# Loading the first w_down block of the first down phase one pair sooner, into the free half of s3

## The chip, the cores and the metric

One core of one Trainium2 chip. The metric is device time in microseconds (us), as the median of several executions; lower is better. The profile's own span leaves out some 1.8 us of that time, so spans are compared with spans and times with times. Engines are called TensorE (PE in the profile, PEld for its weight loads), DVE, ScalarE (ACT), GpSimd (POOL) and SyncE (SP, or SPq for its DMA queue).

## The reference

A gated MLP on 8 x 1024 tokens, with a hidden size of 1024 and an intermediate size of 4096, all float32:

```python
gate = x @ w_gate
up = x @ w_up
gate = 0.5 * gate * (1 + np.tanh(np.sqrt(2 / np.pi) * (gate + 0.044715 * gate ** 3)))
h = gate * up
return (h @ w_down).astype(np.float32)
```

## The kernel before

The kernel works through 8 passes of 1024 tokens in float16, with fast (Strassen-like) matrix products. Pass 0 has 16 "pairs" of gate and up products (56 matmuls of 512 columns in each but the first, which is built differently), then a down phase of 14 "blocks" (32 matmuls of 512 columns each): 7 products, two blocks of w_down operands for each. In pass 0 the even blocks are loaded from a DRAM scratch `wdop`, and the odd blocks are held on chip. The loads use six slots of 4096 columns in `rg`, the ring:

```python
def d_place(p, k):
    if p == 0:
        return (4, 2, 3, 5, 4, 5, 4)[k // 2]     # blocks 0,2,4,6,8,10,12
    return order[0][k % 6]

def d_chunk(p, k):
    if p == 0 and k % 2:
        return half_block(k // 2)
    o = 4096 * d_place(p, k)
    return rg[:, o : o + 4096].rearrange("p (n h) -> p n h", n=8)
```

Slot 4 also holds weight sums of every even pair, so block 0 can be loaded into it only after pair 14. The load is put into the program in pair 15 (`at(k, f, ...)` calls f after the k-th product of the pair):

```python
if i == NP - 1:
    at(1, load_d, p, 2 if p else 0)
```

The tile `s3` (8192 columns) first stages w_down while `wdop` is made; the last stores from it are issued in pass 0 near 174 us. In the down phase it takes the difference a11 - a21, in four quarters r, which the fifth product (P7, from block 8 on) reads:

```python
def hsum(o, a, b, op, r):
    s = slice(4 * r, 4 * r + 4)
    nc.vector.tensor_tensor(hq[o][:, s, :], hq[a][:, s, :], hq[b][:, s, :], op)

for r in range(4):
    sums["P1", 0, r] = [("s3", "a11", "a21", SUB, r)]     # in block 0, after row group r
    sums["P1", 1, r] = [("a21", "a21", "a22", ADD, r)]    # in block 1
```

The same phase makes more operands on DVE: sums for the odd blocks (line 461, stored to `wd_ops` by SyncE) and, for later passes, "quad sums" of w_down (line 278, stored to `wd_quads` by SyncE). It also fetches the next pass's x with four DMA transposes:

```python
if nb == 0 and g == 0 and p + 1 < NPASS:
    ...
    if v == (3 - p if p < FAST - 1 else 0):    # pass 0: in block 6
        transpose_x(p + 1)
...
load_d(p, kc + 6 if p else {0: 8, 6: 10, 8: 12}.get(kc, 14))    # at the end of block kc
```

SyncE issues all of these from one queue, in program order.

## Time and profile before

| what | before |
|---|---|
| time, median of 3 runs | 2256.03 us (2255.78 to 2256.38) |
| span of the profiled run (a run of 2255.39 us) | 2253.6 us |
| TensorE busy | 2245.6 us |
| TensorE's waits in the whole span | 3.8 us |
| of these in the first down phase | 0.6 us, at block 10 |
| block 0's load | issued 197.20, landed 203.6, needed at 209.1 |

TensorE is busy for all but a few microseconds, so a change can save time only where TensorE waits. The lines that show this are in the prediction below.

### The profile page before, as it was taken

How to read it: one execution, taken by the hardware profiler on the slowest of the kernel's cores; microseconds unless marked ns; L12 is line 12 of the kernel's file. 1: busy time of each engine (PE TensorE's matmuls, PEld its weight loads, DVE VectorE, ACT ScalarE, POOL GpSimd, SP SyncE). 2: the span in 40 equal slices, each digit the busy share in tenths (PEclk: the TensorE clock that was granted, in tenths of full speed). 3: DMA queues.
4: the chain of work that ended last, by engine and by line, in shares of the span. 5: the costliest groups of instructions: out<-in, count | busy, mean ns of one | idle time of the engine just before them, and what ended most of it. 6: DMA issues, size and time to landing. Idle time of an engine off the chain costs nothing.

```text
span 2253.6 us, 42764 instructions
## 1 busy us (share of the span) xinstructions
PE 2245.6 (100%) x16616; PEld 1624.2 (72%) x16616; DVE 1565.1 (69%) x2187; ACT 955.4 (42%) x1863; POOL 674.6 (30%) x825
## 2 busy tenths in 40 slices
PE   9999999999999999999999999999999999999999
PEld 4444444444444445888888888888888888888888
DVE  6666458883588755877776677666786667866674
ACT  4443135651365622666125550356404653055520
POOL 1332013330133300555014540255403543044520
PEclk9999999999999999999999999999999999999999
DMA  9898969999999999999998999988998889998886
GB/s 243 164 210 215 289 180 243 258 270 291 243 229 249 281 304 352 332 343 366 302 337 276 320 309 310 324 267 328 314 322 314 283 310 317 322 309 276 285 292 225
DMA packets 309117, 642.46 MB, mean 285 GB/s; under 512 B 79088, under 2 KB 185328, under 8 KB 288368
## 3 DMA queue, kind: packets, MB, share of 16 engines
q1 hardware_dynamic: 254128, 566.57, 73.5%
q0 software_dynamic: 54784, 73.14, 19.5%
q8 instruction: 130, 2.13, 0.4%
q14 instruction: 75, 0.61, 0.1%
HBM read 574.36 MB, written 138.41 MB: 316 GB/s over the span
## 4 chain that ended last, share of the span: by engine, by line
PE 87%; DMA 2%; SPq 1%; DVE 0%; issue 0%; DVEq 0%
PE ps L857 40%; PE ps L1108 20%; PE ps L635 17%; PE ps L1000 10%; DMA wd_quads<-x_sums 1%; SPq L255 0%; DMA ring<-wd_ops 0%; DVE x_sums L278 0%; DVE h_a L932 0%; DVE tmp L1177 0%; SPq L496 0%; DVEq L278 0%; SPq L544 0%
## 5 line engine op out<-in xcount | busy, mean ns | idle before, releaser
L857 PEld LDWEIGHTS <-ring 128*128 128x128 f16 x8320 | 814.1, 98 | 94.4
L834 POOL TENSOR_TENSOR h_a<-tmp 128x256 f16<-128x256 f32 x640 | 468.0, 750 | 840.6 <-ACT tmp L822 833.5
L857 PE MATMUL ps<-x_sums,ring 128*128 128x256 f16 x5760 | 655.8, 273 | 0.0
L819 DVE TENSOR_TENSOR tmp<-tmp,ps 128x512 f32<-128x512 f32 x640 | 414.3, 683 | 147.1 <-PE ps L857 90.2
L635 PEld LDWEIGHTS <-ring 128*128 128x128 f16 x2632 | 257.4, 98 | 311.2 <-DVE ring L360 0.9
L804 ACT COPY tmp<-ps 128x512 f32<-128x512 f32 x520 | 304.2, 585 | 237.0 <-PE ps L857 163.3
L635 PE MATMUL ps<-x_sums,ring 128*128 128x512 f16 x1504 | 340.1, 379 | 0.2 <-DVE ring L360 0.2
L822 ACT ACTIVATE tmp<-tmp 128x256 f32<-128x256 f32 x640 | 263.7, 418 | 173.2 <-DVE tmp L817 79.5
L857 PE MATMUL ps<-x_b,ring 128*128 128x256 f16 x2560 | 305.6, 273 | 0.0
L817 DVE TENSOR_TENSOR tmp<-ps,tmp 128x512 f32<-128x512 f32 x240 | 165.4, 689 | 145.2 <-ACT tmp L804 99.8
L635 PE MATMUL ps<-x_b,ring 128*128 128x512 f16 x1128 | 259.1, 379 | 0.0
L661 POOL TENSOR_TENSOR h_a<-tmp 128x512 f16<-128x512 f32 x94 | 141.1, 1501 | 377.4 <-ACT tmp L659 265.3
L1108 PEld LDWEIGHTS <-h_a 128*128 128x128 f16 x2240 | 219.2, 98 | 25.3
L1000 PE MATMUL ps<-ring,h_a 128*128 128x512 f16 x1024 | 222.3, 379 | 0.6 <-DMA ring<-wd_ops 0.6
L1108 PE MATMUL ps<-ring,h_a 128*128 128x256 f16 x1920 | 216.1, 273 | 0.0
L1000 PEld LDWEIGHTS <-h_a 128*128 128x128 f16 x1152 | 112.6, 98 | 136.8 <-DMA ring<-wd_ops 1.1
L654 DVE TENSOR_TENSOR tmp<-ps,tmp 128x512 f32<-128x512 f32 x188 | 127.3, 685 | 108.0 <-ACT tmp L646 106.5
L1165 ACT ACTIVATE tmp<-ps 128x512 f32<-128x512 f32 x60 | 35.3, 597 | 362.6 <-PE ps L1108 274.6
L1177 DVE SCALAR_TENSOR_TENSOR tmp<-ps,tmp 128x512 f32<-128x512 f32 x120 | 81.1, 690 | 97.5 <-PE ps L1108 66.7
L360 DVE TENSOR_TENSOR ring<-ring 128x1024 f16<-128x1024 f16 x188 | 139.7, 757 | 11.7 <-DMA ring<-in_w_up_dram 7.5
L646 ACT COPY tmp<-ps 128x512 f32<-128x512 f32 x188 | 109.8, 586 | 77.8 <-PE ps L635 77.8
L1108 PE MATMUL ps<-ring,x_sums 128*128 128x256 f16 x1120 | 126.3, 273 | 0.0
(102 smaller groups left out, 1534.0 us busy)
## 6 DMA issues: line engine op xcount, KB each, us to landing
ring<-w_ops SPq DMA_DIRECT2D x480, 512.0 KB, 4.9
ring<-wd_quads SPq DMA_DIRECT2D x110, 1024.0 KB, 6.9
ring<-wd_ops SPq DMA_DIRECT2D x35, 1024.0 KB, 8.2
out_dram<-tmp SPq DMA_DIRECT2D x128, 256.0 KB, 6.6
w_ops<-h_s SPq DMA_DIRECT2D x128, 256.0 KB, 6.8
ring<-in_w_gate_dram POOLq DMA_DIRECT2D x23, 1024.0 KB, 10.6
ring<-in_w_up_dram POOLq DMA_DIRECT2D x23, 1024.0 KB, 17.9
wd_quads<-x_sums SPq DMA_DIRECT2D x131, 128.0 KB, 6.5
```

The source lines that it names most:

```text
L360: nc.vector.tensor_tensor(o, a, b, op)
L635: nc.tensor.matmul(ps(b, w), lhs[:, k], rhs[:, k, :], start=(first and k == 0), stop=(k == KH - 1), skip_group_check=True,)
L654: nc.vector.tensor_tensor(o, ps("b", w), o, ADD)
L661: nc.gpsimd.tensor_tensor(hq[TO[n]][:, i, :], tmp[:, t[n, 1]], tmp[:, t[n, 0]], MUL)
L804: nc.scalar.copy(tmp[:, t[o[1]]], ps_all[:, bank[o[2]]])
L817: nc.vector.tensor_tensor(d, b, a, SUB)
L819: nc.vector.tensor_tensor(d, a, b, ADD if o[4] == "add" else SUB)
L822: nc.scalar.activation(d, d, GELU, scale=GSC)
L834: nc.gpsimd.tensor_tensor(h, tmp[:, t[o[1]], MQ : 2 * MQ], g, MUL)
L857: nc.tensor.matmul(ps_all[:, bank[c], w * MQ : (w + 1) * MQ], lhs[:, w, k], rhs[:, k], start=(first and w == 0 and k == 0), stop=(k == KH ...
L1000: nc.tensor.matmul(ps_all[:, bank[b, g]], lhs[:, j, g * P : (g + 1) * P], dc[:, n, :], start=(first and j == 0), stop=(j == NP - 1), skip_ ...
L1108: nc.tensor.matmul(ps_all[:, bank[c], m * MQ : (m + 1) * MQ], lhs[:, j, m * P : (m + 1) * P], rhs[:, j, :], start=(first and j == 0 and m ...
```

## The change

The intent is to give the first load of the down phase more time. Block 0 no longer goes to ring slot 4 but to the upper half of s3, which staging has left, and its load is put into pair 14. Two of the four a11 - a21 sums write that half, so they move behind block 0. The diff, without the blank lines that it adds:

```diff
     def d_chunk(p, k):
         if p == 0 and k % 2:
             return half_block(k // 2)
+        if p == 0 and k == 0:
+            return hf["s3"][:, 4096:8192].rearrange("p (n h) -> p n h", n=8)
         o = 4096 * d_place(p, k)
...
             if i == NP - 2:
                 order[0] = [0, 1, 4, 2, 3, 5] if p % 2 == 0 else [2, 3, 4, 0, 1, 5]
+                at(2, load_d, p, 0)
                 if p:
-                    at(2, load_d, p, 0)
                     at(3, load_d, p, 1)
-            if i == NP - 1:
-                at(1, load_d, p, 2 if p else 0)
+            if i == NP - 1 and p:
+                at(1, load_d, p, 2)
...
         for r in range(4):
-            sums["P1", 0, r] = [("s3", "a11", "a21", SUB, r)]
-            sums["P1", 1, r] = [("a21", "a21", "a22", ADD, r)]
+            late = p == 0 and r > 1
+            sums.setdefault(("P1", int(late), r % 2 if late else r), []).append(
+                ("s3", "a11", "a21", SUB, r)
+            )
+        for r in range(4):
+            sums.setdefault(("P1", 1, r), []).append(("a21", "a21", "a22", ADD, r))
```

## The prediction

> **What bounds the kernel now.** I read the page's busy list first, then the list of what TensorE waited for, then TensorE's timeline across the first down phase, then the chain of waits there, and last the DVE and SyncE order in it. The busy list, and the whole of TensorE's waits in the kernel (columns: total us, times, longest us):
>
> ```profile
> PE 2245.6 (100%) x16616; PEld 1624.2 (72%) x16616; DVE 1565.1 (69%) x2187; ACT 955.4 (42%) x1863; POOL 674.6 (30%) x825
> ...
> PE ps L1227 <- DVE h_s L1230: 1.6, 1, 1.6
> PE ps L314 <- DVE h_a L304: 0.7, 1, 0.7
> PE ps L1206 <- ACT x_b L317: 0.7, 1, 0.7
> PE ps L1000 <- DMA ring<-wd_ops: 0.6, 1, 0.6
> PE ps L635 <- DVE ring L360: 0.2, 1, 0.2
> ```
>
> The reader is to see that TensorE waits 3.8 us in all (1.6 + 0.7 + 0.7 + 0.6 + 0.2) in a span of 2253.6 us. The change touches only the first down phase (line 1000, pass 0), so all that it can remove from TensorE's path is the one wait of 0.6 us. The question is then whether that wait is the one for the first block. TensorE's timeline says no (start, length, what, idle before):
>
> ```profile
> 206.51 2.75 PE L635 MATMUL ps<-x_b,ring 128*128 128x512 f16 x12
> 209.10 7.07 PE L1000 MATMUL ps<-ring,h_a 128*128 128x512 f16 x32
> 216.00 7.07 PE L1000 MATMUL ps<-x_sums,h_a 128*128 128x512 f16 x32
> ...
> 278.93 20.89 PE L1000 MATMUL ps<-ring,h_a 128*128 128x512 f16 x96 [0.60 <-DMA ring<-wd_ops]
> ```
>
> The first block's 32 matmuls follow the last pair of gate and up with no gap: 206.51 plus 12 matmuls at 0.216 us is 209.10. The idle of 0.60 us stands at 278.93. A block of 32 matmuls takes 216.00 - 209.10 = 6.90 us, and (278.33 - 209.10) / 6.92 = 10.0, so the block that is late is number 10 of 0 to 13, not number 0. Its chain, traced back:
>
> ```profile
> 258.34 0.44 DVE x_sums L278
> ...
> 270.25 0.05 issue
> 270.30 0.02 SPq L544
> 270.32 0.03 issue
> 270.35 8.53 DMA ring<-wd_ops
> 278.88 0.05 issue
> 278.93 27.80 PE ps L1000 x128
> ```
>
> Block 10's load issues at 270.35, behind four transposes (259.17 to 270.25) in SyncE's queue, which stand behind the stores of w_down's quad sums (wd_quads), whose sums DVE makes. That chain goes back, over three landings of wd_quads stores (8.76, 9.70 and 8.77 us), to DVE at 228.96, where DVE had been busy back to back since 209. So DVE's pace from 209 to 232 sets the only wait in this phase.
>
> The first block's own load, in the DMA view of the instant it was issued (197.20; size, us to landing):
>
> ```profile
> ring<-wd_ops SPq DMA_DIRECT2D x1, 1024.0 KB, 6.4
> ```
>
> It landed at 197.2 + 6.4 = 203.6, and was needed at 209.1: 5.5 us to spare.
>
> **What the Trainium skill says.** (1) "TensorE: Matmul & The Clock Gate", section "Step-by-step: what each phase is for", gives 216 ns between back-to-back 512-column matmuls; here 32 take 6.90 us, 215.6 ns each. It agrees, so these blocks run at full pace with nothing to win inside them. (2) "DMA: Bandwidth & Descriptors", section "Anatomy of one DMA", says that DMA engines do not wait on semaphores: the wait is made on the issuing sequencer before dispatch. So a load put earlier in program order can go no sooner than its own waits let SyncE past, and whatever follows in that queue waits with it. The trace agrees: block 10's load goes 0.1 us after the last transpose ahead of it. (3) "SBUF — State Buffer", section "SBUF: two separate sides", says that compute and DMA sides do not contend there. So it should not matter to TensorE whether the block lies in the ring or in s3; no run so far tests that.
>
> **The change part by part.**
> (a) The first load moves from pair 15 to pair 14, and from ring slot 4 to the upper half of s3. Before, it had to wait for pair 14 to end (issued 197.20). Now it waits for the last stores of w_down staging: those issued at 173.28 and 174.48 took 9.9 and 10.4 us, so the last lands at 174.48 + 10.4 = 184.9. The DMA engines are almost empty then (2% from 184.9 to 190.0), and 4.9 us is the fastest this 1 MB load took here, so it should land near 190. The slack grows from 5.5 to about 19 us. TensorE did not wait on it: worth **0 us**.
> (b) Ring slot 4 is free early, so block 8's load no longer waits for block 0 (issued 216.20 before); it goes right behind block 6's, near 209.6. Block 8 is needed at 209.1 + 8 x 6.91 = 264.4, and its load landed at 221.1 even before. Worth 0 us. It takes 1 MB out of 216 to 221 and puts it among three other loads, 205.8 to 218, the first of which is needed only at 222.9.
> (c) TensorE, ScalarE and GpSimd keep their instructions and their order. On DVE no instruction is added, but two of the four a11-a21 sums (128x2048, 1.21 us, spaced 1.14 us) move behind block 0, because they write the half of s3 that block 0 now lies in. DVE's order before:
>
> ```profile
> 213.25 1.21 DVE L461 TENSOR_TENSOR x_sums<-x_sums 128x2048 f16<-128x2048 f16 x1
> 214.38 2.35 DVE L932 TENSOR_TENSOR h_s<-h_a,h_a 128x2048 f16<-128x2048 f16 x2
> 216.65 1.21 DVE L461 TENSOR_TENSOR x_sums<-x_sums 128x2048 f16<-128x2048 f16 x1
> 217.79 1.21 DVE L932 TENSOR_TENSOR h_a<-h_a,h_a 128x2048 f16<-128x2048 f16 x1
> ```
>
> In the changed order the second L461 sum comes up to 214.38 and is done by 215.5. The next is an a11-a21 sum, which may start only when TensorE has finished block 0. When that is seen, the kernel before shows: block 8's load waited for the same event and issued at 216.20. So DVE stands idle 216.20 - 215.51 = **0.69 us**, then runs the same work in nearly the same order: the a21 sums, from 217.79, start at about 217.3 for the first and 0.7 us late from the second on. All that DVE made later, up to 232, is 0.7 us later.
> (d) The consumers on TensorE do not notice. P6 reads the a11 sums from block 4 (236.7), and they begin at 225.94 and end at 231.6, then 232.3; P7 reads s3 from block 8 (264.4), and its last sum ends at about 220.
> (e) The chain to block 10 does notice, since it starts in that DVE stretch. If the landings in it keep their length, block 10's load issues 0.7 us later (271.0), and TensorE's wait grows from 0.6 to 1.3 us.
> The sum: 0 (a) + 0 (b) + 0 (d) + 0.7 at most (e). The chain's links wait on busy DMA queues, and a store that issues 0.7 us later need not land that much later; I take **+0.5 us**, 2256.03 + 0.5 = 2256.5 us.
>
> **The rivals.**
> 1. The transfer was hidden anyway and nothing else moves: 2256.0. For it: no gap at 209.10. Against it: DVE has a new hole, in a stretch that heads the chain.
> 2. The emptier DMA queue helps: with 1 MB gone from 216 to 221, the wd_quads stores land sooner, and block 10 is in time. It can give back at most the 0.6 us: 2255.4. For it: landings of 8 to 10 us for 128 KB are queueing. Against it: the chain's slow stores start at 230, 9 us after that load had landed.
> 3. A new wait on the a21 or a11 sums or on s3 stops TensorE, or SyncE's queue jams on the early load: some us more. Against it: the margins in (d) are 4.4 us (block 4) and more, and nothing stands behind the early load in SyncE's queue until 205.84, 21 us after it can go.
> 4. The intent holds: a wait at the start of the phase goes, worth microseconds. Against it: there is none in the trace, and 45 us (2%) would be twelve times all of TensorE's waits.
>
> **Range and chances.** The runs before lie within 0.6 us (2255.78 to 2256.38). A chain of three queued landings can shift by a microsecond either way, but a gain is capped at 0.6 us while a loss is not. With half a microsecond more for another run of the chip, that gives 2254.8 to 2258.5. Over 2% either way needs a mechanism that no view shows: 0.005 each, and 0.99 for within 2%.
>
> **What would show it.** In the changed profile: block 0's load issued near 185 and landed near 190; no gap at the first line-1000 matmul, as before; block 8's load near 209.6; a DVE idle of about 0.7 us ended by TensorE just after 216; the wait for wd_ops at block 10 at 0.6 to 1.3 us, still TensorE's only wait in the phase. The prediction is wrong if that wait falls to 0 (rival 2), if it exceeds 3 us (a link of the chain was mis-sized), if a wait on DVE shows at line 1000 (rival 3), or if the time falls by more than 0.6 us, which would need a cost that TensorE's waits do not show.

## The result, and the profile after

The changed kernel took 2254.97 us (median of 6 runs, 2254.65 to 2256.40), the kernel before 2255.91 us (6 runs, 2254.71 to 2256.97). The ratio is 0.9997, with a 95% interval of 0.9984 to 1.001: the same. Here and below, a ratio is the mean time of one kernel's runs over that of the other's in the same rounds, so it is not quite the ratio of the medians quoted.

The changed kernel's lines have moved by 2 to 8 (635 is 637, 932 is 935, 1000 is 1008). SyncE's queue (start, length, what), then the size and time to landing of the DMA that it issued between 184 and 186:

```profile
184.99 0.32 SPq L546 DMA_DIRECT2D h_s<-wd_ops  x1
205.90 4.25 SPq L546 DMA_DIRECT2D ring<-wd_ops  x4
```

```profile
h_s<-wd_ops SPq DMA_DIRECT2D x1, 1024.0 KB, 4.9
```

Block 0's load goes at 184.99 and lands at 189.9, 12 us sooner in issue than before. The other four, block 8's among them, go from 205.90 to 210.15. All this is as intended. TensorE's timeline and the one wait of the phase:

```profile
206.57 2.75 PE L637 MATMUL ps<-x_b,ring 128*128 128x512 f16 x12
209.16 7.07 PE L1008 MATMUL ps<-h_s,h_a 128*128 128x512 f16 x32
...
279.64 20.68 PE L1008 MATMUL ps<-ring,h_a 128*128 128x512 f16 x95 [1.25 <-DMA ring<-wd_ops]
```

Block 0 again follows the last pair without a gap, now reading its operand from s3. Its load lands 19 us ahead of that instead of 5.5 us, and TensorE gets nothing for it. The wait at block 10 is there as before, 1.25 us instead of 0.60. This looks like the 0.7 us that I had forecast for it, but DVE's timeline says otherwise:

```profile
209.97 3.42 DVE L935 TENSOR_TENSOR h_s<-h_a,h_a 128x2048 f16<-128x2048 f16 x2
213.31 2.35 DVE L461 TENSOR_TENSOR x_sums<-x_sums 128x2048 f16<-128x2048 f16 x2
215.58 1.21 DVE L935 TENSOR_TENSOR h_s<-h_a,h_a 128x2048 f16<-128x2048 f16 x1
216.72 1.21 DVE L935 TENSOR_TENSOR h_a<-h_a,h_a 128x2048 f16<-128x2048 f16 x1
```

The late a11 - a21 sum starts at 215.58, right behind the sum ahead of it. There is no hole of 0.69 us. Block 0's last matmul ends only at 209.16 + 7.07 = 216.23, so the sum did not wait for the whole block. And the chain to block 10 has the same head as before: its first DVE link starts at 229.02 here and at 228.96 before, the 0.06 us by which the whole phase is shifted. What is longer are links further down (start, length, what):

```profile
230.52 8.70 DMA wd_quads<-x_sums
...
239.28 10.17 DMA wd_quads<-x_sums
...
250.03 8.28 DMA wd_quads<-x_sums
...
270.71 8.88 DMA ring<-wd_ops
279.59 0.05 issue
279.64 27.80 PE ps L1008 x128
```

The landings were 8.76, 9.70, 8.77 and 8.53 us before; they are 8.70, 10.17, 8.28 and 8.88 here, and the transposes between the third and the fourth ended 11.45 us after they began instead of 11.08. The three stores together cancel out (27.23 us before, 27.15 here); the longer wait stands in the transposes (0.37 us more) and in block 10's own landing (0.35 us more). So one profile each cannot tell an effect of the change from the luck of the DMA queues. The experiments had to.

### The profile page after: what moved, and what is told of

Read it like the earlier page. It is cut to its first block, busy times and chain, and to the rows that moved or that the text cites. A ratio compares the mean times of both kernels' runs of the same rounds, so it can differ in the third digit from the quotient of the medians.

```text
span 2254.5 us, 42766 instructions
## 1 busy us (share of the span) xinstructions
PE 2245.6 (100%) x16616; PEld 1624.1 (72%) x16616; DVE 1559.6 (69%) x2187; ACT 956.7 (42%) x1863; POOL 682.6 (30%) x825
## 4 chain that ended last, share of the span: by engine, by line
PE 87%; DMA 2%; SPq 1%; DVE 0%; issue 0%; DVEq 0%
PE ps L860 40%; PE ps L1116 20%; PE ps L637 17%; PE ps L1008 10%; DMA wd_quads<-x_sums 1%; SPq L255 1%; DMA ring<-wd_ops 0%; DVE x_sums L278 0%; DVE h_a L935 0%; DVE tmp L1185 0%; SPq L496 0%; DVEq L278 0%; SPq L546 0%
## 5 line engine op out<-in xcount | busy, mean ns | idle before, releaser
L663 POOL TENSOR_TENSOR h_a<-tmp 128x512 f16<-128x512 f32 x94 | 148.2, 1576 | 368.5 <-ACT tmp L661 262.7
L1008 PE MATMUL ps<-ring,h_a 128*128 128x512 f16 x992 | 215.3, 379 | 1.2 <-DMA ring<-wd_ops 1.2
```

Of the source, the lines that this page charges most:

```text
L663: nc.gpsimd.tensor_tensor(hq[TO[n]][:, i, :], tmp[:, t[n, 1]], tmp[:, t[n, 0]], MUL)
L1008: nc.tensor.matmul(ps_all[:, bank[b, g]], lhs[:, j, g * P : (g + 1) * P], dc[:, n, :], start=(first and j == 0), stop=(j == NP - 1), skip_ ...
```

## The experiments

The theory now: (1) block 0's load was hidden, and making it more so is worth nothing; (2) the reordered sums leave no hole in DVE, because a sum waits only for the last matmul that reads its own quarter of s3; (3) the wait at block 10 hangs on DVE's pace, on landings that vary, and on the place of its load in SyncE's queue, none of which the change moves. The rivals: the early block gives something that block 10's later wait took back; or the reordering lengthens the chain. Medians, with the kernel before in the same rounds ("none" and the other waits are those of the one profiled run):

| run | us | before, us | ratio (95% interval) | wait at block 10 in the profile |
|---|---|---|---|---|
| before_t | 2255.53 | 2255.79 | 0.9997 (0.9985 to 1.001) | none |
| after_t | 2254.67 | 2255.79 | 0.9996 (0.9983 to 1.0008) | none |
| sums_only | 2255.49 | 2255.79 | 0.9999 (0.9985 to 1.0012) | none |
| hole | 2256.00 | 2255.79 | 1.0001 (0.9988 to 1.0013) | 0.68 us |
| before_t2 | 2254.57 | 2255.05 | 0.9997 (0.9985 to 1.001) | none |
| after_t2 | 2254.66 | 2255.05 | 0.9998 (0.9985 to 1.001) | none |
| b0_late | 2262.90 | 2255.05 | 1.0034 (1.0021 to 1.0048) | 0.34 us |
| dve_plus | 2262.74 | 2255.05 | 1.0034 (1.0019 to 1.005) | 5.59 us |
| dve_two | 2259.00 | 2254.79 | 1.002 (1.0004 to 1.0035) | 2.22 us |
| before_again | 2255.33 | 2254.79 | 1.0 (0.9988 to 1.0013) | 0.17 us |
| after_again | 2255.76 | 2254.79 | 1.0005 (0.9992 to 1.0017) | 0.49 us |

All outputs are right. By the rule that a difference under 2% counts as none, every row is the same. The interval of a ratio is some 0.0013 wide to each side, or 2.9 us: of the differences in time, only those of b0_late, dve_plus and dve_two are clear of it, and what is smaller is read from the traces. The rows stem from three calls, each on another chip: the first four, the next four, and the last three.

### before_t: block 10's load ahead of the transposes

The kernel before, with the transposes moved from block 6 to block 7, behind block 10's load:

```diff
+                    if p == 0 and v == 3 and nb == 1 and g == 0:
+                        transpose_x(p + 1)
                     if nb == 0 and g == 0 and p + 1 < NPASS:
...
-                        if v == (3 - p if p < FAST - 1 else 0):
+                        if p and v == (3 - p if p < FAST - 1 else 0):
                             transpose_x(p + 1)
```

> The kernel before, with one thing moved: SyncE issues block 10's load ahead of the four transposes instead of behind them. My theory (the only wait in the first down phase is block 10's, because its load stands behind the transposes): the load issues near 259 and lands near 268, ten us before it is needed; the wait of 0.6 us at block 10 goes to 0, TensorE's waits in the whole kernel are then about 3.0 us, and every run lies near the fastest so far (span near 2252.9, 2254.7 us), with less spread. Rival (the wait only moves, since the transposes are now later): a wait of 0.5 us or more appears at the start of pass 1 or at block 12, and the time stays at 2255.9.

SyncE's queue in the order of issue, and TensorE at block 10:

```profile
259.45 0.40 SPq L544 DMA_DIRECT2D ring<-wd_ops  x1
259.90 14.54 SPq L255 DMA_TRANSPOSE x_b<-x_half  x4
```

```profile
278.07 20.88 PE L1000 MATMUL ps<-ring,h_a 128*128 128x512 f16 x96
```

The load goes 11 us sooner than in the kernel before and lands 7.8 us later, at 267.3, which is 10.8 us before its use. Block 10 starts with no idle ahead of it. TensorE's waits in the whole span come to 3.3 us, in a span of 2252.7 us, and none is on a block. That block 10's load was late because of its place in the queue is thereby shown. The forecast of less spread failed in these rounds: four of the five runs took 2255.05 to 2255.68, one 2254.50. No profile fell on one of the longer runs.

### after_t: the same move in the changed kernel

The same edit on the changed kernel.

> The changed kernel with the same move of the transposes. My theory (the early first block is worth nothing at all, before or after): same time as the kernel before with that move, within 0.3 us, near 2254.7, no wait on a block. Rival (the early block gives something that block 10's later wait took back): with that wait gone this one is faster than the kernel before with the move, by 0.5 us or more.

No wait on a block either. But the median was 0.86 us below before_t's, which by the letter of what I had written speaks for the rival. The traces did not: from block 0's first matmul to pass 1's first takes 305.70 - 209.00 = 96.70 us in before_t and 305.86 - 209.16 = 96.70 us in after_t. The chains show the same, in one unbroken piece of 448 matmuls (first before_t, then after_t):

```profile
209.17 96.69 PE ps L1000 x448
```

```profile
209.32 96.69 PE ps L1008 x448
```

So both were run again.

### before_t2 and after_t2: both once more, on another chip

> Again the kernel before with block 10's load ahead of the transposes, because its median was 0.86 us above that of the changed kernel with the same move, though neither trace shows a wait on a block. My theory (the gap is run to run scatter that sits outside the first down phase): together with the run of the same name before, the two kernels' means lie within 0.5 us of each other, and the phase from its first matmul to the first of pass 1 takes 96.70 us in both. Rival (the early block is worth 0.5 us or more once block 10 is out of the way): the gap comes again, 0.5 us or more.

> Again the changed kernel with the same move. My theory: mean within 0.5 us of the other's, phase 96.70 us. Rival: lower by 0.5 us or more again.

2254.57 us (2254.54 to 2254.72) and 2254.66 us (2254.59 to 2254.81). The gap has gone, and the order is reversed. The phase takes 305.80 - 209.11 = 96.69 us in the one and 305.78 - 209.08 = 96.70 us in the other. By their means over both pairs of rounds the two are 0.17 us apart (2254.94 and 2254.77, worked out from the ten runs of each). With block 10's wait out of the way, the early block 0 is still worth nothing that can be seen; the rival in which block 10 took back a gain falls, on the traces above all: TensorE has no idle in this phase in any of the four profiles. On this chip the move also did what I had expected of the spread: 0.2 us, where the kernel before ran from 2254.58 to 2256.68.

### sums_only: the reordered sums alone

The kernel before, with only the last hunk of the change. Block 0 stays in the ring.

> The kernel before with only the second part of the change: two of the four a11-a21 sums move behind block 0; block 0 stays in the ring and its load stays where it was. My theory after seeing the changed kernel's trace (the reordering leaves no hole in DVE, and the difference of 1.25 against 0.60 us at block 10 is chance in the landings): DVE has no idle over 0.2 us between 210 and 232, the wait at block 10 is anywhere from 0 to 1.3 us, time 2254.7 to 2256.9. Rival (the reordering lengthens the chain by its other order of the quad sums): block 10's wait is at 1.2 us or more and the time is 0.5 us or more above the kernel before in the same rounds.

DVE is busy without an idle from 210 to 232, and the wait at block 10 did not occur: its load was issued at 270.92, 0.57 us later than in the kernel before, yet landed in time. The median is 0.3 us below the kernel before. The reordering costs nothing that this run shows; the rival's wait of 1.2 us and time of 0.5 us above did not come.

### hole: the two late sums swapped

The changed kernel, with the sum on the last quarter of s3 ahead of that on the third:

```diff
-            sums.setdefault(("P1", int(late), r % 2 if late else r), []).append(
+            sums.setdefault(("P1", int(late), 3 - r if late else r), []).append(
```

> The changed kernel with its two late sums swapped, so that the first of them writes the last quarter of s3, which block 0's very last matmuls read. My corrected step (a sum waits only for the last matmul that reads its own quarter, not for the whole block): here DVE does stand idle, about 0.5 to 0.7 us until just after 216.1, and in the changed kernel it did not. What follows in the chain is 0.5 to 0.7 us later at its head near 229; block 10's wait grows by at most that, to a time from 2254.7 to 2257. Rival (the whole block is waited for in either order, and DVE was late for another reason): no idle appears here that the changed kernel did not have.

```profile
213.35 2.35 DVE L461 TENSOR_TENSOR x_sums<-x_sums 128x2048 f16<-128x2048 f16 x2
216.36 1.23 DVE L935 TENSOR_TENSOR h_s<-h_a,h_a 128x2048 f16<-128x2048 f16 x1 [0.66 <-issue]
```

Here is the hole that I had forecast for the changed kernel: 0.66 us, against none with the other order. Block 0 is 4096 columns of s3. The third quarter of s3 is its first half, which each group of 8 matmuls reads in its first four. So the last matmul to read it ends four matmuls (0.86 us) before the block does, at about 216.23 - 0.86 = 215.4 in the changed kernel, some 0.2 us before DVE gets to the sum at 215.58. The last quarter is read to the block's end, which is 209.19 + 7.07 = 216.26 here, 0.1 us before the sum starts. The head of the chain came 0.8 us later (its DVE sum at 229.73, against 228.95 in the changed kernel), block 10's load was issued at 271.65 and landed in 7.4 us, and the wait was 0.68 us. On the time (ratio 1.0001) a hole of that size cannot be seen.

### b0_late: block 0's load made late

The kernel before, with block 2's load put ahead of block 0's in SyncE's queue:

```diff
             if i == NP - 1:
-                at(1, load_d, p, 2 if p else 0)
+                if p:
+                    at(1, load_d, p, 2)
+                else:
+                    at(10, load_d, p, 2)
+                    at(11, load_d, p, 0)
...
-                            for k in range(3, 6) if p else (2, 4, 6):
+                            for k in range(3, 6) if p else (4, 6):
```

> The kernel before, with block 0's load made late on purpose: block 2's load (which must wait for pair 15's last use of its ring slot, near 205.6) is put ahead of it in SyncE's queue, so block 0's load issues near 206.2 instead of 197.2. My theory (the change is worth nothing because the load had 5.5 us to spare; a load later than that slack costs its excess on TensorE, one for one): block 0 lands near 214, TensorE stands idle 4 to 5.5 us before the first line-1000 matmul, block 10's wait is swallowed by that (0), and the time is 3.5 to 5 us above the kernel before. Rival (a wait at the start of the phase is made up for later in the phase, so that no placement of this load matters): the idle shows but the time grows by less than 1.5 us.

TensorE's timeline, and its granted clock in three stretches after it (stretch, its length, busy time and count of PE, PEld, DVE, ACT and POOL, then the granted clock, the share of the DMA engines and GB/s):

```profile
215.26 8.49 PE L1004 MATMUL ps<-ring,h_a 128*128 128x512 f16 x32 [6.05 <-DMA ring<-wd_ops]
223.59 7.07 PE L1004 MATMUL ps<-x_sums,h_a 128*128 128x512 f16 x32
```

```profile
215.26:217.00 1.74, 1.74 (x5) 0.62 (x5) 1.74 (x3) 0.00 (x0) 0.00 (x0) 0.50 1.01 428
217.00:218.00 1.00, 1.00 (x4) 0.37 (x3) 1.00 (x2) 0.00 (x0) 0.00 (x0) 0.50 1.01 426
219.00:220.00 1.00, 1.00 (x7) 0.47 (x5) 1.00 (x2) 0.00 (x0) 0.00 (x0) 1.00 0.06 25
```

The load was issued 9.0 us later, behind another 1 MB, and landed 9.06 us after that, at 215.2. Of the delay (8.96, and 2.66 more for the longer landing) the slack of 5.5 us was to cover its part: 11.62 - 5.5 = 6.1, and TensorE stood idle 6.05 us. That settles what the slack was. The idle was a little longer than the 4 to 5.5 us expected, and block 10 kept a wait of 0.34 us where I expected none. The cost was more than I had expected, 7.9 us by the medians: after the idle the clock was at 0.50 for some 3 us, and block 0 took 223.59 - 215.26 = 8.33 us instead of 6.90. Idle 6.05 and 1.42 of slow matmuls are 7.5 us. The Trainium skill, "TensorE: Matmul & The Clock Gate", section "HAM oscillation — how this bites in real kernels", warns of idle gaps over about 3.4 us for this reason; the trace agrees.

### dve_plus: more DVE work at the head of the chain

The kernel before, with each of the two L461 sums at the start of the down phase made three times over:

```diff
-            (0, 1): [lambda: half_sum(1, 0)],
+            (0, 1): [lambda: half_sum(1, 0)] * 3,
...
-            (0, 3): [lambda: half_sum(1, 1)],
+            (0, 3): [lambda: half_sum(1, 1)] * 3,
```

> The kernel before, with four more DVE sums of 128x2048 (1.14 us apart, 4.6 us in all; each repeats a sum just made, so the result is right) between the s3 sums, at the head of the chain to block 10. My theory (block 10's wait hangs on DVE's pace there, through the quad sums and SyncE's queue): the chain's head near 229 comes 4.6 us later, the wait at block 10 grows from 0.6 to between 3 and 5.5 us, and the time by 2.5 to 4.9 us. Rival (the links are DMA landings that end when the queues drain, whatever DVE does): block 10's wait stays below 1.5 us and the time within 1 us of the kernel before.

```profile
284.00 23.24 PE L1000 MATMUL ps<-ring,h_a 128*128 128x512 f16 x96 [5.59 <-DMA ring<-wd_ops]
307.08 7.07 PE L1000 MATMUL ps<-x_sums,h_a 128*128 128x512 f16 x32
```

The quad sum that began at 230.01 in the kernel before begins at 235.14 here, 5.1 us later. Block 10's load is issued at 275.56, 5.2 us later, and its wait grows by 5.0 us. So the chain does run from DVE through SyncE to block 10, nearly one for one, and the rival that the queues swallow the delay falls. The two lines of this, the quad sum on DVE and the issue on SyncE:

```profile
235.14 0.41 DVE L278 TENSOR_TENSOR x_sums<-x_sums,spare 128x512 f16<-128x512 f16 x1
```

```profile
275.56 0.53 SPq L544 DMA_DIRECT2D ring<-wd_ops  x1
```

The wait came out just above the 3 to 5.5 us expected, and the time grew by clearly more than the 2.5 to 4.9 us. Again a lowered clock followed the idle (columns as in b0_late):

```profile
287.00:288.00 1.00, 1.00 (x4) 0.42 (x3) 0.00 (x0) 0.00 (x0) 0.00 (x0) 0.50 1.04 382
289.00:290.00 1.00, 1.00 (x6) 0.44 (x5) 0.00 (x0) 0.00 (x0) 0.00 (x0) 1.00 1.08 402
```

It was 0.50 from 284 to 288, and the stretch up to block 13 took 307.08 - 284.00 = 23.08 us instead of 20.73. That is 2.35 us on top of the 5.0, 7.3 in all of the 7.7 us that the medians show.

### dve_two: half of that dose

Two more sums instead of four (`* 2` instead of `* 3` in the same places).

> Half the dose of the run with four extra DVE sums: two extra sums of 128x2048, 2.3 us of DVE at the head of the chain. That run cost 7.5 us where I had expected at most 4.9, because an idle of 5.6 us on TensorE was followed by 4.6 us at a granted clock of 0.50. My theory (the cost is the idle plus, for idles of several us, a spell at half clock): block 10's wait is 1.5 to 3.5 us, the clock stays at 1.00 after it, and the time is 1 to 3 us above the kernel before. Rival (any growth of DVE's work here costs about 1.6 times itself): the time is 3.5 us or more above, with a spell of lowered clock.

```profile
280.66 20.89 PE L1000 MATMUL ps<-ring,h_a 128*128 128x512 f16 x96 [2.22 <-DMA ring<-wd_ops]
```

In the profiled run the wait was 2.22 us, the clock stayed at 1.00 after it, and the time was 2257.12 us, 2.3 above the kernel before. The quad sum began at 232.66, 2.65 us later than in the kernel before, and block 10's load was issued at 273.15, 2.8 us later: again nearly one for one, at half the dose. One more run took 2257.13. Two others took 2260.88 and 2261.31 us, each with a mean clock of 0.999 where the first two had 1.000. So neither expectation held as a whole. A spell at half clock like that of dve_plus, which cost 2.35 us, would make up little more than half of the extra 4 us of these two runs; the profile caught neither of them, and the last digit of the mean clock proves nothing by itself: one run of the kernel before is listed with 0.999 at 2254.64 us. What made those two runs longer stays open.

### before_again and after_again: a second profile of each

> The kernel before, unchanged, for a second profile of it. My theory (block 10's wait is chance between 0 and 1.3 us in both kernels, as the landings of the wd_quads stores fall): median 2254.6 to 2256, the wait at block 10 somewhere in 0 to 1.3 us, not again 0.60. Rival (the wait is a fixed 0.6 us in this kernel and a fixed 1.25 us in the changed one): 0.6 again.

> The changed kernel, unchanged, for a second profile in the same rounds. My theory: median within 0.6 us of the kernel before, wait at block 10 anywhere in 0 to 1.3 us. Rival (the change lengthens or shortens the chain): 1.25 us again and a median 0.6 us above, or the other way round.

The wait at block 10 was 0.17 us in the kernel before (0.60 in the first profile) and 0.49 us in the changed one (1.25). So its size is not fixed in either kernel. It was the larger one in the changed kernel both times, but the part of the chain that the change could lengthen was not longer as a rule: counted from block 0's first matmul, block 10's load was issued after 61.25 and 61.87 us in the kernel before, and after 61.55 and 61.36 us in the changed one. What differed was the landing of that load itself, 8.53 and 7.49 us against 8.88 and 8.32; it was 7.40 us in hole, which has the change too. The times are at the limit of what can be told: the kernel before, run under another name in the same rounds as itself, came out 0.54 us above itself by the medians, and the changed kernel 0.97 us above it. By the letter of what I had expected (within 0.6 us) that failed, and the rival had the time right and the wait wrong; against before_again, in the same rounds, it is 0.43 us. One of its five runs took 2258.74 us; the other four took 2255.66 to 2256.31. None of the 33 runs of the kernel before in these comparisons was so long (2257.20 at most). The mean clock of this one run was 0.999, as in the two long runs of dve_two, and 1.000 in the other four; it was not profiled. One run is too few to say that the change makes it likelier, and that stays open.

## Why the prediction was right or wrong

"The same" was right. The number was in range, but near its lower end: 2256.5 us with a range of 2254.8 to 2258.5 was forecast, 2254.97 us measured, at a ratio of 0.9997. The small rise that I forecast did not show; the median was 0.94 us below the kernel before. A fall of more than 0.6 us was one of my own signs of being wrong. Here it cannot be told from scatter: the kernel before alone ran from 2254.71 to 2256.97 us in these rounds, and after_again came out 0.97 us above. That the range held the result is owed to its width (its ends do not follow from the terms named beside it: 2256.03 - 0.6 - 0.5 is 2254.9, and for the upper end no sum is given). By its own steps:

- **(a), the load was hidden, 0 us: right.** Issue at 184.99 and landing at 189.9, against "184.9" and "near 190". Block 0 had no wait before or after, and its matmuls take 6.91 us from s3 (209.16 to 216.07) against 6.90 from the ring. b0_late shows the other side: when the load came later than the 5.5 us of slack could cover, TensorE waited for the rest.
- **(b), block 8's load goes early, 0 us: right.** It was issued with block 6's, by 210.15, and no wait came of it.
- **(c), the hole of 0.69 us in DVE: wrong.** The step that failed is the sentence that the late sum "may start only when TensorE has finished block 0". It waits for the last reader of its own quarter, 0.86 us earlier (215.4), and DVE got there later than that (215.58), so its idle was 0 instead of 0.69 us. Swapping the two sums (hole) brought the hole back at 0.66 us, so the reasoning was right for the last quarter and I applied it to the third.
- **(d), P6 and P7 notice nothing: right.** No wait on DVE shows at line 1008 in the phase.
- **(e), the chain carries a DVE delay to block 10: right as a mechanism, with nothing to carry.** dve_plus moved block 10's load by 5.2 us for 5.1 us of DVE. With no hole, the term of +0.5 us should have been 0. The wait of 1.25 us in the changed profile, inside my forecast of 0.6 to 1.3, came from the transposes and block 10's own landing; that it matched was luck, and the second profiles have 0.17 us before and 0.49 us after.
- **Rival 1**, in which nothing moves and the time stays at 2256.0, was the true account, within what the times can tell. **Rival 2** was not seen: the wait did not go, and the three stores took 27.15 us together instead of 27.23. **Rivals 3 and 4** show nowhere: no new wait, and none at the phase's start to remove.
- **The scatter was under-thought.** I took 0.6 us from three runs, and read a profile whose own run, 2255.39 us, was faster than all three. Over all rounds the kernel before ran from 2254.58 to 2257.20 us (33 runs). Part of this is block 10's wait. Part is not: before_t has no such wait in its profile and still had four runs of 2255.05 to 2255.68 us on one chip and five of about 2254.6 us on another. Where those go was not found. One kept trace shows a place outside the phase: in before_again TensorE takes 194.4 us for the gate and up products of pass 1 (306.14 to 500.57), in before_t 193.4 us (305.70 to 499.08), and two of its short waits there end with ScalarE's copies at line 646.

The move of the transposes gives the best medians, 2254.57 and 2254.66 us, with or without the change. Against the kernel before that is a ratio of 0.9997 to 0.9998 with intervals that include 1, so it is not called faster.

## What to carry to other kernels

Before moving a load earlier, subtract its landing from the first use: 5.5 us of slack on a load that nothing waits for means that more slack buys nothing, and the chain of waits names the load that is late instead (here one stuck behind transposes in an in-order queue). When a buffer is lent to something else for a while, look at which of its parts is read last, since the order in which the parts are taken back decides whether an engine stalls. And one profile each is not enough to lay 0.65 us of a wait at a change's door: take a second profile of the same kernel first.

## What the Trainium skill lacked or had wrong

- "TensorE: Matmul & The Clock Gate", section "HAM oscillation — how this bites in real kernels", gives the idle gap that brings the clock down (over about 3.4 us), and the traces agree at 5.59 and 6.05 us idle, which were followed by a clock of 0.50 and cost 2.35 and 1.42 us beyond the idle. It lacks a case of a single gap below that figure: here 2.22 us idle left the clock at 1.00 in the profiled run, while two of four runs of the same kernel took 3.8 to 4.2 us more, with a mean clock of 0.999. Those two were not profiled, so neither the length of their gap nor a lowered clock as the reason is shown.
- "DMA: Bandwidth & Descriptors", section "Anatomy of one DMA", fits 2.0 us plus bytes over 436 GB/s, for the GpSimd path, which for a 128 KB store would be an estimate of 2.3 us. Where the DMA engines were less busy (a share of 0.63 from 219 to 223 us in the kernel before), three such stores, issued from SyncE, took 2.4 us in the median, close to that. The stores that make up the chain here, issued from 230 us on, after two stores of 1 MB at 225.88 and 226.67, took 8.28 to 10.17 us to land in the changed kernel's profile, and differed by up to 0.5 us from those of the kernel before. I found no figure on that page for a landing behind queued work.
